# Two plain columns fewer and one Strassen step more in a two-layer diffusion backbone, with first columns in three passes and the softmax scale in the queries

## The chip, the cores and the metric

The kernel runs on one core of a Trainium2 chip. The metric is the device time of one execution in microseconds (us). Its engines work in parallel and each executes its own instruction stream: TensorE (PE) multiplies, VectorE (DVE) and ScalarE (ACT) work elementwise, GpSimd (POOL) issues some of the DMA transfers here, SyncE (SP) issues most. Semaphores order the engines among each other.

## The reference

Two layers. Each is a half-step gated FFN, a token mixing (a bidirectional mLSTM beside a multi-head latent attention), and a second half-step FFN; 256 context tokens and 256 latent tokens go through the same weights, D = 1024, hidden width 2816.

```python
def _swiglu(h, w_up, w_dn):
    a, b = jnp.split(h @ w_up, 2, axis=-1)
    return (jax.nn.silu(a) * b) @ w_dn
...
    def one(qi):
        s = jnp.einsum('bqhd,bkhd->bhqk', qi, k).astype(jnp.float32) * scale
        pr = jax.nn.softmax(s, axis=-1).astype(v.dtype)
        return jnp.einsum('bhqk,bkhd->bqhd', pr, v)
...
        mx = [m[:, None, :] for m in jnp.split(jax.nn.silu(c) @ w_ada[l] + b_ada[l], N_MOD, axis=-1)]
...
        x = x + 0.5 * mx[2] * _swiglu(_modulate(_rmsnorm(x, g_n1[l]), mx[0], mx[1]), w_ff1_up[l], w_ff1_dn[l])
```

## The kernel before

Everything is fp32. A product of two fp32 matrices is made of three matmuls on high and low parts: `hh`/`hl` are the parts of the normed activations, `wh`/`wl` those of a weight unit. ACT copies the unit `st` to `wh` (rounded), DVE subtracts to get `wl`. Four buffers exist for `wh` and `wl` each (`WB`), six for `st` (`STB`). A 256-wide matmul serves one of the two streams (CTX, LAT), a 512-wide one both.

The up projection of an FFN has 22 columns of 128 for each of the two halves a and b. In two of the four FFNs (`SEVEN`: layer 0's second, layer 1's first; function `ff7`) most columns are done two at a time as one *step*: a block product of a 2 x 2 matrix of weights (a11, a12, a21, a22) with the two streams' activations, by seven products instead of eight (class `Step`). Product r multiplies a combination of weights by a combination of activations. The combinations of activations (`d7`, their parts `dh` and `dl`) are made once per FFN by `differences`, on DVE (subtractions and low parts) and ACT (high parts). The combinations of weights are made per step: products 5, 6 and 7 add a further block onto the tile that is there by an accumulating DMA from POOL (`more`), and product 3 adds two tiles on DVE (`st_b += st_c`, where `st_c` is a21+a22+a11, product 6's tile). The products of one step are interleaved with two of the next, and the first step begins with (0,5), (0,1), (0,2), then (0,6), (1,5), (0,7), (0,3), where (t, r) is product r of step t. Their matmuls go into PSUM tiles `rA`, `rB`, `rC`, 24 of 256 each.

The first columns of an FFN come as plain ones. `up_early` does two of them stream by stream, as soon as the norm of a stream is there (LAT, then CTX); between them PE sums squares for the norm of the second stream (`nps`). Then `up` does the remaining plain columns (512 wide), and the steps follow. Finished columns go in chunks (`CHUNKS`: plain columns, steps) to the down projection (`dn`).

A queue of *ada* pieces (the modulation of later sub-layers: a weighted sum per row on DVE) is spread over the FFN by `drip`. A helper `high_priority(offset)` lets a scheduler put instructions earlier in their engines' streams; the streams themselves are then fixed, and each engine waits at an instruction until its semaphores are there.

Attention scores come as PSUM tiles `sc`; DVE takes the maximum of a row (L1470), scales it (L1471), ACT takes exp with the scale as its factor (L1475), DVE the reciprocal, ACT the division, and PE transposes the probabilities (`pT`).

Of the kernel before, what the change touches and what calls it, by code (L numbers as in the profile page):

```python
# [16 lines left out]
P = 128  # L17
D = 1024
KB = D // P
T = 512  # L20
# [24 lines left out]
FIRST = 4  # L45
STEPS = (FB - FIRST) // 2
CHUNKS = ((4, 1), (0, 4), (0, 4))
# [98 lines left out]
def body(ctx, tc, A):  # L146
# [178 lines left out]
    def silu2(out, src):  # L325

        tanh_half(out, src)
        V.scalar_tensor_tensor(out, out, 1.0, src, ALU.add, ALU.mult)

# [7 lines left out]
    def silu_rows(streams):  # L337

        res = {}
        for s in streams:  # L340
            for q in range(2):
# [3 lines left out]
                silu2(res[s, q], v)  # L345
# [243 lines left out]
    def up_early(part, jobs):  # L589
# [3 lines left out]
        banks = [(psum("pa"), psum("pb")) for _ in jobs]  # L593
        for b in (0, 1):
            for (lhs, _), pair_ in zip(jobs, banks):
                for i, ps in enumerate(pair_):
                    sl = slice(i * P, (i + 1) * P)
                    for k in range(KB):
                        for a in (0, 1) if b == 0 else (0,):
                            TE.matmul(  # L600
                                ps[:, :w], lhs[k][a][:, sl], hp[k][b],
                                start=b + k + a == 0, stop=b == 1 and k == KB - 1, skip_group_check=True,
                            )
                    flush()
        for (_, dst), (pa, pb) in zip(jobs, banks):
            gated(pa, pb, w, dst)
# [220 lines left out]
    def ff7(l, f, queue, after):  # L827
# [10 lines left out]
        for c, (first, n) in enumerate(CHUNKS):  # L838
# [20 lines left out]
            for st in mine:  # L859
# [23 lines left out]
    def mix(l, after):  # L883
# [530 lines left out]

        def mla_proj(p):
# [4 lines left out]
            run(split_gen([(a, b[:, :T], c[:, :T]) for a, b, c in zip(ps, his, los)]))  # L1420
# [4 lines left out]
            S.activation(z[:, :qn], ps[:, :qn], AF.Copy)  # L1425
# [26 lines left out]
        scale = (NOPE + ROPE) ** -0.5  # L1452

        def mla():
            def scores(p, hd, s):
# [322 lines left out]
```

## Time and profile before

| | |
|---|---|
| three runs | 2347.57, 2348.99, 2350.08 us; median 2348.99 |
| the profiled execution | 2347.62 us, span 2345.8 us, mean granted clock 0.993 |
| matmuls | 15414, PE busy 98% of the span |
| the two FFNs with steps | from 1021.8 to about 1375 and from 1375.7 to about 1734 |
| mixing of layer 0, of layer 1 | about 415 to 1000, 1734.6 to about 2141 |

A busy share is that of the whole span; a wait of PE is read from the list of waits and from the timeline around it. The lines L... are those of the kernel before.

### The profile page before, as it was taken

The numbers are of one execution on the slowest core, as the hardware profiler recorded it, in microseconds if no ns is written. First come the engines' busy times: TensorE is split into PE (matmuls) and PEld (weight loads), VectorE is DVE, ScalarE is ACT, GpSimd is POOL, SyncE is SP. The second block draws the span as 40 slices with busy tenths as digits, with TensorE's granted clock in tenths as the row PEclk, the third lists the DMA queues.
The fourth block names the chain that finished last, engine by engine and source line by source line (L and its number), as shares of the span: only waits on it lengthen the run. The fifth ranks groups of instructions, "written<-read, shape, count | busy, mean of one in ns | idle before, by whom it ended". The sixth has DMA issues, their size and how long they took to land.

```text
span 2345.8 us, 39386 instructions
## 1 busy us (share of the span) xinstructions
PE 2291.2 (98%) x15414; PEld 2083.6 (89%) x15414; DVE 1695.6 (72%) x3463; ACT 1089.9 (46%) x1776; POOL 144.1 (6%) x298
## 2 busy tenths in 40 slices
PE   8999999999999999999999999999999899999998
PEld 4888888888888888889999999999998798999998
DVE  6777777797477745468795868986878776776755
ACT  6322223567545433254443554443546564555443
POOL 1112110000010000000101000100000000000000
PEclk9999999999999999999999999999999999999999
DMA  9547444312122223436776637786732233365763
GB/s 337 200 155 239 153 150 151 102 57 73 55 81 73 73 77 94 128 105 185 203 218 166 193 89 212 213 253 183 239 94 83 91 100 99 99 183 161 245 206 105
DMA packets 116825, 347.15 MB, mean 148 GB/s; under 512 B 13854, under 2 KB 16158, under 8 KB 116638
## 3 DMA queue, kind: packets, MB, share of 16 engines
q1 hardware_dynamic: 99902, 286.94, 38.1%
q0 software_dynamic: 16736, 57.68, 10.9%
q8 instruction: 121, 1.98, 0.3%
q14 instruction: 66, 0.54, 0.1%
HBM read 341.42 MB, written 3.15 MB: 147 GB/s over the span
## 4 chain that ended last, share of the span: by engine, by line
PE 92%; DVE 4%; ACT 1%; DMA 1%; issue 1%; SPq 0%; DVEq 0%; ACTq 0%
PE dn L268 12%; PE dn L518 9%; PE rA L775 8%; PE p L292 4%; PE p L293 4%; PE p L294 4%; PE rB L775 4%; PE pa L294 3%; PE pa L292 3%; PE pa L293 3%; PE pb L292 3%; PE pb L294 3%; PE pb L293 3%; PE pv L268 2%; PE rC L775 2%; PE pb L600 2%
## 5 line engine op out<-in xcount | busy, mean ns | idle before, releaser
L246 ACT ACTIVATE wh<-st 128x1024 fp32r<-128x1024 f32 (+3 forms) x396 | 391.6, 993 | 641.3 <-PE pb L293 120.3
L248 DVE TENSOR_TENSOR wl<-st,wh 128x1024 fp32r<-128x1024 f32 (+3 forms) x396 | 449.6, 1139 | 201.3 <-ACT wh L246 198.0
L759 ACT ACTIVATE wh<-st 128x1024 fp32r<-128x1024 f32 x126 | 133.0, 1058 | 126.0 <-PE dn L518 54.2
L404 DVE SCALAR_TENSOR_TENSOR ada<-ada,cs 128x512 f32<-128x512 f32 x256 | 168.4, 686 | 18.7 <-DMA ada<-ada 18.7
L293 PE MATMUL p<-hl,wh 128*128 128x256 f32 (+1 forms) x536 | 179.4, 335 | 0.0
L292 PE MATMUL p<-hh,wh 128*128 128x512 f32 (+1 forms) x512 | 173.5, 339 | 0.0
L294 PE MATMUL p<-hh,wl 128*128 128x512 f32 (+1 forms) x512 | 172.5, 337 | 0.0
L760 DVE TENSOR_TENSOR wl<-st,wh 128x1024 fp32r<-128x1024 f32 x126 | 153.8, 1222 | 22.0 <-ACT wh L759 21.8
L512 DVE SCALAR_TENSOR_TENSOR x<-dn,mod,x 128x256 f32<-128x256 f32 x168 | 75.5, 479 | 96.8 <-PE dn L268 48.9
L404 DVE SCALAR_TENSOR_TENSOR junk<-ada,cs 128x512 f32<-128x512 f32 x192 | 124.2, 686 | 1.9 <-DMA ada<-ada 1.9
L294 PE MATMUL pb<-hh,wl 128*128 128x512 f32 (+1 forms) x352 | 120.6, 343 | 0.0
L294 PE MATMUL pa<-hh,wl 128*128 128x512 f32 (+1 forms) x352 | 120.6, 343 | 0.0
L292 PE MATMUL pa<-hh,wh 128*128 128x512 f32 (+1 forms) x352 | 120.6, 343 | 0.0
L292 PE MATMUL pb<-hh,wh 128*128 128x512 f32 (+1 forms) x352 | 120.6, 343 | 0.0
L293 PE MATMUL pa<-hl,wh 128*128 128x512 f32 (+1 forms) x352 | 120.4, 342 | 0.0
L293 PE MATMUL pb<-hl,wh 128*128 128x512 f32 (+1 forms) x352 | 120.4, 342 | 0.0
L293 PEld LDWEIGHTS p<-hl,wh 128*128 128x128 f32 x536 | 100.7, 188 | 10.8
L294 PEld LDWEIGHTS p<-hh,wl 128*128 128x128 f32 x512 | 96.1, 188 | 11.3
L292 PEld LDWEIGHTS p<-hh,wh 128*128 128x128 f32 x512 | 96.1, 188 | 10.9
L268 PE MATMUL dn<-hi,wh 128*128 128x512 f32 (+1 forms) x286 | 102.5, 360 | 0.0
L268 PE MATMUL dn<-hi,wl 128*128 128x512 f32 (+1 forms) x286 | 102.3, 358 | 0.0
L268 PE MATMUL dn<-lo,wh 128*128 128x512 f32 (+1 forms) x286 | 102.1, 358 | 0.0
(436 smaller groups left out, 7067.8 us busy)
## 6 DMA issues: line engine op xcount, KB each, us to landing
st<-wall SPq DMA_DIRECT2D x372, 512.0 KB, 3.7
ada<-ada SPq DMA_DIRECT2D x176, 256.0 KB, 5.9
ada<-ada POOLq DMA_DIRECT2D x112, 256.0 KB, 3.5
st<-wall POOLq DMA_DIRECT2D x54, 512.0 KB, 5.8
st<-wall SPq DMA_DIRECT2D x56, 384.0 KB, 3.4
st<-wall SPq DMA_DIRECT2D x32, 320.0 KB, 3.0
cb<-cc SPq DMA_DIRECT2D x14, 256.0 KB, 6.2
x<-xT SPq DMA_DIRECT2D x8, 256.0 KB, 5.6
```

What stands on the lines that cost most here:

```text
L246: S.activation(hi[:, :n], st[:, :n], AF.Copy)
L248: V.tensor_tensor(lo[:, :n], st[:, :n], hi[:, :n].bitcast(F32), ALU.subtract)
L268: TE.matmul(ps, lhs[k][a][:, lsl], rhs[k][b][:, rsl], start=i == 0, stop=i == 3 * n - 1)
L292: TE.matmul(ps, a, b, start=first, stop=False)
L293: TE.matmul(ps, a, bl, start=False, stop=False)
L294: TE.matmul(ps, al, b, start=False, stop=final_)
L404: V.scalar_tensor_tensor(o, st, 0.5, cb[s, q], ALU.mult, ALU.mult, accum_out=dst)
L512: V.scalar_tensor_tensor(xs[nb][:, cols], ps[:, pcols], mod(l, s, g, nb), xs[nb][:, cols], ALU.mult, ALU.add)
L518: TE.matmul(ps[:, s * HALF : (s + 1) * HALF], lhs[k][a], rhs[k][s][b], start=start and i == 0, stop=stop and i + 1 == len(todo), skip_grou ...
L759: S.activation(hi, st, AF.Copy)
L760: V.tensor_tensor(lo, st, hi.bitcast(F32), ALU.subtract)
L775: mm = TE.matmul(ps[:, p * HALF : (p + 1) * HALF], w[x][:, p, k], hx["op", r][k][y], start=new and i == 0, stop=i + 1 == len(todo), skip_g ...
```

## The change

Five edits. In the two FFNs with steps, two plain columns (`FIRST`) are left instead of four, all of them done by `up_early`, and ten steps instead of nine do the rest. `up_early` goes over its two columns in three passes (`hh` with `wh`, `hh` with `wl`, `hl` with `wh`) and keeps a and b of a column in one PSUM tile `pab`; the start of the mixing gets the same order. The weights by which `drip` spreads the ada pieces are changed. The softmax scale moves into the copies that make the query parts, so the scaling of the maximum (48 instructions) goes away, and reductions, exps and divisions get a raised priority. Silu of the conditioning goes through ACT's Silu table instead of tanh and a DVE operation.

```diff
-FIRST = 4
+FIRST = 2
 STEPS = (FB - FIRST) // 2
-CHUNKS = ((4, 1), (0, 4), (0, 4))
+CHUNKS = ((2, 2), (0, 4), (0, 4))
...
-                silu2(res[s, q], v)
+                silu(res[s, q], v)
...
-                V.scalar_tensor_tensor(o, st, 0.5, cb[s, q], ALU.mult, ALU.mult, accum_out=dst)
+                V.scalar_tensor_tensor(o, st, 1.0, cb[s, q], ALU.mult, ALU.mult, accum_out=dst)
...
-        banks = [(psum("pa"), psum("pb")) for _ in jobs]
-        for b in (0, 1):
-            for (lhs, _), pair_ in zip(jobs, banks):
-                for i, ps in enumerate(pair_):
-                    sl = slice(i * P, (i + 1) * P)
-                    for k in range(KB):
-                        for a in (0, 1) if b == 0 else (0,):
...
+        banks = [psum("pab") for _ in jobs]
+        order = [(a, b, n, i, k) for a, b in ((0, 0), (1, 0), (0, 1)) for n in range(len(jobs)) for i in (0, 1) for k in range(KB)]
+        for a, b, n, i, k in order:
+            TE.matmul(
+                banks[n][:, i * w : (i + 1) * w], jobs[n][0][k][a][:, i * P : (i + 1) * P], hp[k][b],
+                start=a + b + i + k == 0, stop=b + i == 2 and k == KB - 1, skip_group_check=True,
+            )
...
-                queue.run(min(1.0, done[0] / (STEPS + len(CHUNKS) * KB * 2 / 7 - 0.6)))
+                queue.run(min(1.0, done[0] / (STEPS * 0.6 + len(CHUNKS) * KB * 0.5 - 0.6)))
...
-                    drip(1 / 7)
+                    drip(0.6 / 7)
...
-                drip(2 / 7)
+                drip(0.5)
...
-            run(split_gen([(a, b[:, :T], c[:, :T]) for a, b, c in zip(ps, his, los)]))
+            run(split_gen([(a, b[:, :T], c[:, :T]) for a, b, c in zip(ps, his, los)], scale))
...
-                    mx.append(sp.tile([P, 3], F32, tag="mx", name="mx", bufs=8))
-                    V.reduce_max(mx[qb][:, 0:1], ps[qb], AX.X, negate=True)
-                    V.tensor_scalar(mx[qb][:, 0:1], mx[qb][:, 0:1], scale, None, ALU.mult)
-                    pump()
+                    with tc.high_priority(offset=SOON):
+                        mx.append(sp.tile([P, 3], F32, tag="mx", name="mx", bufs=8))
+                        V.reduce_max(mx[qb][:, 0:1], ps[qb], AX.X, negate=True)
+                        pr.append(act(F32, "pr")[:, :nk])
+                        S.activation(pr[qb], ps[qb], AF.Exp, bias=mx[qb][:, 0:1], accum_out=mx[qb][:, 1:2])
+                    pump(2)
```

In the changed kernel L600 is L591, L577/L580 (gating) are L572/L575, L695 to L697 (differences) L687 to L690, L682 (low part) L674, L752 (`st_b += st_c`) L744, L760 (`wl` of a product) L752, L775 (products) L767, L464 (`nps`) L459.

**The start of layer 0's second FFN on PE.** Of before, from the last pairs on the first early column to the first product; `pa` and `pb` are the two halves of a column, `hh`/`hl` and `wh`/`wl` the parts of activations and weights:

```order
L600 MATMUL pa<-hh,wh 128x256
L600 MATMUL pa<-hh,wl 128x256
L600 MATMUL pa<-hl,wh 128x256 x6
L464 MATMUL nps<-sq,ones 128x256 x2
L600 MATMUL pb<-hh,wh 128x256
...
L600 MATMUL pb<-hl,wh 128x256 x8
L292 MATMUL pa<-hh,wh 128x512
L293 MATMUL pa<-hl,wh 128x512
...
L294 MATMUL pb<-hh,wl 128x512
L775 MATMUL rC<-dh,wh 128x256
```

And of the change, from the end of the mixing to the first matmul of product (0,5):

```order
L268 MATMUL dn<-lo,wh 128x256
L591 MATMUL pab<-hh,wh 128x256 x16
L591 MATMUL pab<-hh,wl 128x256 x16
L591 MATMUL pab<-hl,wh 128x256 x6
L459 MATMUL nps<-sq,ones 128x256 x2
L591 MATMUL pab<-hh,wh 128x256 x16
L591 MATMUL pab<-hh,wl 128x256 x16
L591 MATMUL pab<-hl,wh 128x256 x26
L591 MATMUL pab<-hh,wh 128x256 x32
L591 MATMUL pab<-hh,wl 128x256 x32
L591 MATMUL pab<-hl,wh 128x256 x32
L767 MATMUL rC<-dh,wh 128x256
```

Ahead of `nps` stand 38 matmuls of the early columns (before: 16 in pairs and 6); behind `up_early` the 96 matmuls of 512 (L292 to L294) are gone, and product (0,5), which goes into `rC`, follows at once.

**The same place on DVE.** The numbers tell buffers apart. Of before, from the last gating of `up_early`: `st_10107`, `wl_10111` belong to product (0,5), `st_10147`, `wl_10150` to (0,1):

```order
L577 TENSOR_TENSOR sg_9920<-sg_9920,pb_9818 128x256
L695 TENSOR_TENSOR d7_9925<-h7_9514,h7_9667 128x512
L760 TENSOR_TENSOR wl_10111<-st_10107,wh_10110 128x1024
L580 TENSOR_TENSOR hl_9814<-sg_9920,hl_9814 128x256
L682 TENSOR_TENSOR dl_9928<-d7_9925,dh_9927 128x512
L695 TENSOR_TENSOR d7_9931<-h7_9521,h7_9674 128x512
L682 TENSOR_TENSOR dl_9934<-d7_9931,dh_9933 128x512
L696 SCALAR_TENSOR_TENSOR d7_9937<-d7_9925,h7_9681 128x512
L760 TENSOR_TENSOR wl_10150<-st_10147,wh_10149 128x1024
L682 TENSOR_TENSOR dl_9940<-d7_9937,dh_9939 128x512
L696 SCALAR_TENSOR_TENSOR d7_9943<-d7_9931,h7_9688 128x512
```

And of the change: `wl_9923` is product (0,5)'s, `wl_9962` is (0,1)'s, `wl_9995` is (0,2)'s and `wl_10027` is (0,6)'s; `st_9919` is `st_c` and `st_9992` is `st_b`:

```order
L752 TENSOR_TENSOR wl_9923<-st_9919,wh_9922 128x1024
L752 TENSOR_TENSOR wl_9962<-st_9959,wh_9961 128x1024
L752 TENSOR_TENSOR wl_9995<-st_9992,wh_9994 128x1024
L572 TENSOR_TENSOR sg_9865<-sg_9865,pab_9767 128x256
L575 TENSOR_TENSOR hl_9765<-sg_9865,hl_9765 128x256
L744 TENSOR_TENSOR st_9992<-st_9992,st_9919 128x1024
L572 TENSOR_TENSOR sg_9870<-sg_9870,pab_9768 128x256
L752 TENSOR_TENSOR wl_10027<-st_9919,wh_10026 128x1024
L687 TENSOR_TENSOR d7_9875<-h7_9472,h7_9615 128x512
L575 TENSOR_TENSOR hl_9766<-sg_9870,hl_9766 128x256
L674 TENSOR_TENSOR dl_9878<-d7_9875,dh_9877 128x512
L687 TENSOR_TENSOR d7_9881<-h7_9479,h7_9622 128x512
```

The three `wl` of the first products, the addition `st_b += st_c` of (0,3) (L744) and `wl` of (0,6) now stand ahead of the first difference (L687); before, the first difference stood ahead of the first `wl` of a step, and the same addition (L752) came 15 rows behind it. L744 waits for the landing of POOL's accumulating transfer for (0,6), and that transfer for `wl_9923`.

## Rows read from the trace of the kernel before

**Rows 1.** The page, parts 1 and 4: busy time, share and instructions; shares of the chain that ended last.

```profile
PE 2291.2 (98%) x15414; PEld 2083.6 (89%) x15414; DVE 1695.6 (72%) x3463; ACT 1089.9 (46%) x1776; POOL 144.1 (6%) x298
...
PE 92%; DVE 4%; ACT 1%; DMA 1%; issue 1%; SPq 0%; DVEq 0%; ACTq 0%
```

**Rows 2.** The list of PE's waits: who waited for whom, us in total, times, longest.

```profile
PE pT L1489 <- ACT pr L1475: 6.4, 1, 6.4
...
PE rB L775 <- DVE rB L812: 2.7, 2, 2.5
```

**Rows 3.** The chain that ended last, 1045 to 1160: start, us, what.

```profile
1048.63 0.93 PE pb L600 x8
...
1071.72 0.24 PE pb L294
1071.96 2.84 PE rC L775 x24
...
1083.23 2.84 PE rC L775 x24
...
1134.12 2.83 PE rA L775 x24
...
1153.85 2.83 PE rA L775 x24
```

**Rows 4.** Timeline of PE from 1014: start, us, instruction [idle before and its releaser].

```profile
1023.85 0.39 PE L600 MATMUL pa<-hh,wh 128*128 128x256 f32 x1 [0.84 <-ACT hh L672]
...
1027.86 0.78 PE L600 MATMUL pa<-hl,wh 128*128 128x256 f32 x2 [1.15 <-DVE hl L673]
1028.60 1.13 PE L464 MATMUL nps<-sq,ones 128*128 128x256 f32 x4
```

**Rows 5.** Windows: us, busy time of PE, PEld, DVE, ACT, POOL, granted clock, DMA, GB/s.

```profile
1383.00:1386.00 3.00, 3.00 (x15) 2.67 (x14) 0.64 (x2) 1.65 (x4) 0.00 (x0) 0.60 0.81 207
...
1820.00:1840.00 20.00, 13.55 (x84) 12.17 (x83) 19.56 (x42) 10.45 (x21) 1.52 (x3) 0.83 0.46 143
...
1836.00:1838.00 2.00, 2.00 (x8) 1.71 (x8) 1.97 (x8) 2.00 (x6) 0.00 (x0) 0.50 0.36 145
```

**Rows 6.** Timeline of ACT from 1044.

```profile
1047.26 2.01 ACT L246 ACTIVATE wh<-st 128x1024 fp32r<-128x1024 f32 x2 [3.33 <-PE pb L600]
...
1058.90 0.64 ACT L681 ACTIVATE dh<-d 128x512 fp32r<-128x512 f32 x1 [2.00 <-DVE d L695]
```

**Rows 7.** Timeline of DVE from 1044.

```profile
1057.24 0.42 DVE L580 TENSOR_TENSOR hl<-sg,hl 128x256 fp32r<-128x256 f32 x1
...
1058.18 0.69 DVE L695 TENSOR_TENSOR d<-h,h 128x512 f32<-128x512 f32 x1
1059.57 0.69 DVE L682 TENSOR_TENSOR dl<-d,dh 128x512 fp32r<-128x512 f32 x1 [0.70 <-ACT dh L681]
1060.18 0.69 DVE L696 SCALAR_TENSOR_TENSOR d<-d,h 128x512 f32<-128x512 f32 x1
1061.70 1.23 DVE L760 TENSOR_TENSOR wl<-st,wh 128x1024 fp32r<-128x1024 f32 x1 [0.84 <-ACT wh L759]
...
1069.65 1.22 DVE L752 TENSOR_TENSOR st<-st 128x1024 f32<-128x1024 f32 x1
```

**Rows 8.** Timeline of POOL from 1056.

```profile
1063.22 0.84 POOL L732 DMA_DIRECT2D st<-wall  x1 [4.50 <-DVE wl L760]
```

**Rows 9.** Line L732 alone (54 accumulating transfers): from issue to landing.

```profile
DMA to landing us min/median/max: 5.2/5.8/11.4
```

**Rows 10.** Timeline of DVE from 1826, layer 1's attention.

```profile
1830.83 0.69 DVE L1470 TENSOR_REDUCE mx<-sc 128x1 f32<-128x512 f32 x1
...
1831.94 0.69 DVE L1470 TENSOR_REDUCE mx<-sc 128x1 f32<-128x512 f32 x1
...
1834.76 0.21 DVE L1471 TENSOR_SCALAR mx<-mx 128x1 f32<-128x1 f32 x2
```

**Rows 11.** Timeline of ACT from 1828.

```profile
1834.94 0.69 ACT L1475 ACTIVATE pr<-sc,mx 128x512 f32<-128x512 f32 x1 [5.51 <-DVE mx L1471]
```

More of the change, by code (lines that the diff above doesn't have):

```diff
@@ L323, in silu @@
         S.activation(out, src, AF.Silu)
-    def silu2(out, src):
-        tanh_half(out, src)
-        V.scalar_tensor_tensor(out, out, 1.0, src, ALU.add, ALU.mult)
     mods = {}
@@ L592, in up_early @@
         w, hp = part.stop - part.start, hpairs(part)
-        banks = [(psum("pa"), psum("pb")) for _ in jobs]
-        for b in (0, 1):
-            for (lhs, _), pair_ in zip(jobs, banks):
-                for i, ps in enumerate(pair_):
-                    sl = slice(i * P, (i + 1) * P)
-                    for k in range(KB):
-                        for a in (0, 1) if b == 0 else (0,):
[L600 to L606, printed above, removed]
+        banks = [psum("pab") for _ in jobs]
[5 more added lines that the diff above has]
+            )
+            if k == KB - 1:
+                flush()
+        for (_, dst), ps in zip(jobs, banks):
+            gated(ps[:, :w], ps[:, w : 2 * w], w, dst)
     def ff(l, f, streams, queue, after):
@@ L1412, in mlstm @@
             heads[NH - 1].turn()
+        scale = (NOPE + ROPE) ** -0.5
         def mla_proj(p):
@@ L1424, in mla_proj @@
             z = act(F32, "qz")
-            S.activation(z[:, :qn], ps[:, :qn], AF.Copy)
+            S.activation(z[:, :qn], ps[:, :qn], AF.Copy, scale=scale)
             lhs = units([("ukv", l, p)], UW, 2)
@@ L1450, in mla_proj @@
             ready["mla", p] = pairs2(his, los), qr, [k[1:] for k in kn], [v[1:] for v in mv]
-        scale = (NOPE + ROPE) ** -0.5
         def mla():
@@ L1468, in scores @@
                 for qb in range(2):
[L1469 to L1479 removed]
+                    with tc.high_priority(offset=SOON):
[4 more added lines that the diff above has]
+                    pump(2)
+                for qb in range(2):
+                    with tc.high_priority(offset=SOON):
+                        V.reciprocal(mx[qb][:, 2:3], mx[qb][:, 1:2])
+                        S.activation(pr[qb], pr[qb], AF.Copy, scale=mx[qb][:, 2:3])
                     pump()
@@ L1534, in mix @@
             h_ = hpairs(cols)
+            outs = [(pk[:, cols], 1, two[1])]
             if cols == LAT or not last:
-                for b in range(3):
-                    mm3(pq[b][:, cols.start - q0 : cols.stop - q0], lhs[b // 2], h_, lsl=two[b % 2], late=True)
-                    if b == 1:
+                outs = [(pq[b][:, cols.start - q0 : cols.stop - q0], b // 2, two[b % 2]) for b in range(3)] + outs
+            for a, b in ((0, 0), (1, 0), (0, 1)):
+                for n, (o, u, sl) in enumerate(outs):
+                    for k in range(KB):
+                        TE.matmul(
+                            o, lhs[u][k][a][:, sl], h_[k][b],
+                            start=a + b + k == 0, stop=b == 1 and k == KB - 1, skip_group_check=True,
+                        )
+                    if n == 1:
                         flush()
-            mm3(pk[:, cols], lhs[1], h_, lsl=two[1], late=True)
         sq = lowrank_squares([t[:, :qn] for t in pq], qn)
@@ L1619, in body @@
     sc = cp.tile([P, 16], F32, name="sc")
-    silu2(sc, vecs[:, c0 : c0 + 16])
-    V.tensor_scalar(sc, sc, 0.5, None, ALU.mult)
+    silu(sc, vecs[:, c0 : c0 + 16])
     squares = [act(F32, "sq")[:, :T] for _ in range(KB)]
```

6 lines of the change are left out of this document (removed).

## Prediction

> **What bounds the kernel now.** I read the page first. TensorE (PE) is busy 98% of the span and carries 92% of the chain that ended last; VectorE (DVE) is busy 72% [rows 1]. So a term counts when it removes matmul time from PE, or when it opens or closes a wait of PE; work of the other engines counts only where PE ends up waiting for it. I then took the list of PE's waits. It is short: the largest single one is a transpose in layer 1's attention, 6.4 us, and the products of the FFNs wait for the rB addition 2.7 us in all [rows 2]. Almost nothing is idle, so the change can give little, and the question is which waits it creates. The chain and the timelines at the first of the two FFNs with seven products (it starts at 1021.8) give the rest.
>
> The profiled execution took 2347.62 us, 1.4 below the median of 2348.99. The sum is made against 2347.62 and the forecast is set against the median, so 1.4 is added at the end. About 0.2%, 4.7 us, is what a measurement of this kernel can tell from no change.
>
> **The change, part by part.**
>
> *A step for two plain columns.* The two plain columns run from the end of `up_early` (1048.63 + 0.93 = 1049.56) to the first product at 1071.96: 22.4 us for 96 matmuls of 512. One step is seven products, 1134.12 to 1153.85 = 19.73 us, 0.117 us a matmul (2.80 / 24) [rows 3]. Two FFNs: 2 x 2.67 = -5.3 us.
>
> *Three passes at the start of an FFN.* PE waits 0.84 us for hh, then 1.15 for hl, and reaches the norm's sums of the other stream (`nps`) at 1028.60 [rows 4]. When `nps` can start is set by its squares, not by PE. Before, 22 matmuls of the early columns stand ahead of `nps`; now 38 do (PE's order above), so 16 more, 16 x 0.117 = 1.9 us, are done while PE would wait. I take off 0.25 for the table load that now stands before the last hh on ScalarE (ACT): -1.65 each, -3.3 us for the two FFNs. Bounds: 0 if the wait only moves, -1.9 each if all is gained. In the second FFN the wait is followed by a spell at a mean granted clock of 0.60, part of it at the lower level of 1.2 GHz: 15 matmuls in 3 us instead of the 1.75 that they need [rows 5]. If PE stays busier it goes: -1.3, with 0 as the other bound.
>
> *The cover that the two plain columns gave.* This is the term that decides. Write E for the end of `up_early`. Before, DVE and ACT had the 22.4 us of the plain columns to build the differences (`d7`, `dh`, `dl`) and the step's weights (`wh`, `wl`). Now product (0,5) stands right behind `up_early`, and needs at E what was built over the next 22 us.
>
> Its weights can't be early. All four `wh` buffers hold the two early columns, and the row of before in which ACT converts the next ones waits 3.33 us for PE and starts at 1047.26, 2.3 before E [rows 6]. So wh of (0,5) is done about E-1.1, and its wl, 1.23 us on DVE, at E+0.2 [rows 7]. Then comes what the order shows: behind it stand wl of (0,1) and (0,2), two small gating operations, and at once the addition `st_b += st_c` of product (0,3) (L744), ahead of the differences. That addition waits for POOL's accumulating transfer of (0,6) into the same `st_c`, and this transfer may begin only when wl of (0,5) has read `st_c`. In the trace POOL issues 0.29 us after that wl ends (1061.70 + 1.23, then 1063.22) [rows 7, 8], and a transfer of this line lands 5.2 to 11.4 us after its issue, 5.8 in the median [rows 9]. I take the median: the lowest and the highest bound it. So: issue E+0.5, landing E+6.3, addition 1.22 to E+7.5, one gating operation 0.4 to E+7.9, wl of (0,6) 1.23 to E+9.1. Only then does d7 of (0,5) start: 0.6 for d7, 0.64 for dh on ACT, the rest of a gating operation and dl 0.69 to E+11.1, then the second half. From one d7 to the next takes 2.0 us when dl has to wait for dh (1058.18 to 1060.18) [rows 7]: second dl at E+13.0. Half of the 24 matmuls are still to come, 1.4: (0,5) ends at E+14.5 instead of E+2.8.
>
> (0,1), (0,2), (0,6) follow at 2.8 each, to E+22.9, no longer waiting. (1,5) waits again: its wl stands behind four more pairs of d7 and dl (4 x 2.0, to E+21.0), two d7 of product 4 (1.2), one low part (0.7), the addition into a7 (0.7) and takes 1.23, to E+24.9. (1,5) ends at E+27.7. In the trace of before it ends 14.1 after the first product begins (1083.23 + 2.84 - 1071.96) [rows 3]. Delay 13.6, which PE never regains, since it is the bound. What is behind the waiting addition on DVE is thus everything that PE needs next; POOL and SP have nothing late. The second FFN has the same order of rows. 2 x 13.6 = +27.2. Bounds: landing at 5.2 makes each 0.6 less, at 11.4 5.6 more; a DVE that is not held by the addition is a rival below.
>
> *ada pieces.* The queue of modulation pieces is spread by weights; products had 9 of 15.3 and have 6 of 17.4 now, so less of it falls where DVE also makes the weights. The 2.7 us for rB should go [rows 2]: -2.7, 0 at the other end (the stretches of the down projection get more of it, and there PSUM banks lie between DVE and PE).
>
> *Softmax.* The 6.4 us are one transpose that needs a PSUM bank that exp frees. The exp waits 5.51 us for the scaling of the maximum: both maxima are there at 1832.63, the two scalings run at 1834.76, behind other work of a DVE that is busy 19.56 of 20 us [rows 5, 10, 11]. Now no scaling stands between, and the first exp could begin at the end of its own reduction, 1830.83 + 0.69 = 1831.52 instead of 1834.94: -3.4. The bounds are 0 (another operation stands there) and -8 (the wait and the spell at 0.50, 1.2 GHz, behind it, 8 matmuls in 2.0 us [rows 5]). Layer 0's attention has only small waits: -1, between -4 and +2, since raised priority of reductions and exps also pushes something else back.
>
> *Mix start, silu, scale.* In layer 0, 7 matmuls fewer stand ahead of `nps`: 7 x 0.117 = +0.8; 0 in layer 1. Silu by table instead of tanh, and the scale in a copy that runs anyway, sit on ACT and DVE away from PE's waits: 0, within 0.5 either way.
>
> Sum: -5.3 - 3.3 - 1.3 + 27.2 - 2.7 - 3.4 - 1.0 + 0.8 = +11.0. 2347.62 + 11.0 + 1.4 = 2360.0.
>
> By the Trainium skill (DMA: Bandwidth & Descriptors, the section Anatomy of one DMA) a transfer from GpSimd takes about 2.0 us and its bytes at 436 GB/s, an estimated 3.2 us for these 512 KB. The stall would be 2.6 shorter in each FFN and the time about 2355; no transfer of this line landed under 5.2 in the trace, and the page's fit is of plain copies, so the trace's median stays in the sum.
>
> **The rivals.**
>
> *A. DVE is not held by the waiting addition.* If it went on to d7 behind it, d7 would start at about E+3.6 (two more wl and two gating operations after E+0.2), the second dl would be at E+7.6, and (1,5) would end near E+22.2: a delay of 8 each, 16 in all, against -16.2 of the other terms: 2349, no change. Against it: the dl at 1059.57 waits 0.70 us for ACT while the next d7 at 1060.18, whose inputs were complete, stands behind it [rows 7]. The Trainium skill (Perfetto Trace Analysis, Tensor Engine Instruction) calls ACT, DVE and GPSIMD "strict FIFO"; by that rule, with which the row agrees, this rival is left only as a chance that the wait itself is shorter than I think.
>
> *B. The stall is hidden, and the kernel is faster.* Its place is the same: conversion and differences would have to be over before E. Without any stall the sum is -16.2, so 2332.8; it ends faster by over 0.2% if the stall is below 5.7 us in each FFN. That needs wh of (0,5) to start some 10 us sooner; the ACT row that waits for PE's last reading of a buffer speaks against it [rows 6].
>
> *C. The stall is worse.* Landing at 11.4 [rows 9], or the rB addition ahead of (0,3) late behind ada pieces, adds 5 to 6 us per FFN: above 2371.
>
> **How the numbers follow.** Forecast 0.68, A 0.12, B 0.12, C 0.08. The time is the forecast's, 2360. The range leaves out B and C: from 2345, which takes in A, to 2371. Faster: B and a quarter of A, 0.15. Within 0.2%: the rest of A and a little of the forecast's lower edge, 0.11. Slower: 0.74.
>
> **What would show it.** In the profile after: a wait of PE at the first L767 in both FFNs for dh or dl, 9 to 13 us in all, and one of 1 to 3 us at (1,5) for wl; a DVE idle of 2 to 4 us ahead of L744, put down to a DMA; no PE wait for rB; the transpose's 6.4 shortened. If PE passes from `up_early` to rC with under 3 us idle, the decisive term is wrong and B holds. The prediction also fails if the attention stretches move by more than 8 us either way.

## The result and the profile after

The changed kernel takes 2372.78 us (median of 2371.60, 2371.81, 2373.76 and 2375.98), against 2348.90 for the kernel before in the same series: ratio 1.0095, 95% interval [1.0083, 1.0107], which is 22.3 us (19.5 to 25.1); the medians are 23.9 apart. The sign was forecast, the size was not: +11.0 in the sum, and 2371 as the upper end of the range.

The profiled execution took 2373.76 us (span 2372.1, mean granted clock 0.985, was 0.993). The page, parts 1 and 4, as in [rows 1]:

```profile
PE 2301.6 (97%) x15558; PEld 2099.4 (89%) x15558; DVE 1696.2 (72%) x3413; ACT 1099.7 (46%) x1788; POOL 149.1 (6%) x304
...
PE 88%; DVE 4%; issue 3%; DMA 2%; ACT 2%; POOL 0%; DVEq 0%; SPq 0%; POOLq 0%; ACTq 0%
```

PE has 10.4 us more of busy time, and its share of the chain falls from 92 to 88%. The busy time can't come from the work: it has two plain columns fewer and one step more in each of two FFNs, which is less matmul time. The same work was done at a lower clock in more places. The list of PE's waits, against [rows 2], has the idle part:

```profile
PE rC L767 <- ACT dh L673: 19.5, 2, 9.9
...
PE pT L1480 <- ACT pr L1465: 3.0, 1, 3.0
PE rA L767 <- ACT sa L795: 2.8, 2, 1.6
...
PE rB L767 <- DVE rB L804: 0.4, 1, 0.4
```

Two new waits of nearly 10 us stand at the first product of the two FFNs with steps; the transpose's wait halved, and the one for rB (2.7) is down to 0.4. Cut at the starts of the same stages on PE (first matmul of a kind in the trace), the two spans differ so:

| stretch on PE | before | after | difference |
|---|---|---|---|
| span's start to first early column, layer 0's first FFN | 42.9 | 44.2 | +1.3 |
| its early columns | 24.2 | 26.2 | +2.0 |
| rest of that FFN | 348.0 | 348.0 | 0.0 |
| mixing of layer 0 | 606.7 | 607.5 | +0.8 |
| layer 0's second FFN (steps) | 353.9 | 366.5 | +12.6 |
| layer 1's first FFN (steps) | 358.9 | 366.4 | +7.5 |
| mixing of layer 1 | 412.1 | 413.9 | +1.8 |

Where the stall stands, PE has only two waits between the early columns and the end of (1,5). Timeline of PE, from 1052:

```profile
1063.41 0.58 PE L767 MATMUL rC<-dh,wh 128*128 128x256 f32 x1 [9.87 <-ACT dh L673]
...
1075.85 0.39 PE L767 MATMUL rA<-dh,wh 128*128 128x256 f32 x1 [1.60 <-ACT sa L795]
```

`up_early` ends at 1063.41 - 9.87 = 1053.54; this is E. The timeline of POOL, the one of DVE and the one of ACT behind it:

```profile
1053.87 0.85 POOL L724 DMA_DIRECT2D st<-wall  x1 [25.49 <-DVE wl L752]
```

```profile
1056.80 0.43 DVE L575 TENSOR_TENSOR hl<-sg,hl 128x256 fp32r<-128x256 f32 x1 [0.48 <-ACT hl L574]
1059.40 1.23 DVE L744 TENSOR_TENSOR st<-st 128x1024 f32<-128x1024 f32 x1 [2.17 <-DMA st<-wall]
...
1060.88 1.22 DVE L752 TENSOR_TENSOR wl<-st,wh 128x1024 fp32r<-128x1024 f32 x1
1062.01 0.69 DVE L687 TENSOR_TENSOR d<-h,h 128x512 f32<-128x512 f32 x1
```

```profile
1059.40 1.06 ACT L751 ACTIVATE wh<-st 128x1024 fp32r<-128x1024 f32 x1 [2.36 <-DMA st<-wall]
...
1062.73 0.63 ACT L673 ACTIVATE dh<-d 128x512 fp32r<-128x512 f32 x1 [1.32 <-DVE d L687]
```

The reader sees the chain of the forecast link by link. The transfer is issued at E+0.3 and both engines go on at 1059.40, E+5.9, with DVE idle for 2.17 us at an addition whose result PE needs six products later. d7, whose inputs are complete, starts behind it at E+8.5. In layer 1 the same row of PE stands at 1428.12 with 9.67 us.

The stall costs more than its two waits. PE comes out of the first one at half clock, and the 24 matmuls of (0,5) take 5.1 us where they took 2.84 before:

```profile
1064.00:1067.00 3.00, 2.86 (x13) 2.86 (x14) 1.98 (x4) 0.92 (x2) 0.00 (x0) 0.50 0.89 310
```

The rest of the 26 us between the two spans is in no list of waits. Windows, columns as in [rows 5]; the first piece is the kernel before (early columns of layer 0's first FFN, start of its mixing), the second the changed kernel in the same stages (they stand 1.3 and 3.4 us later there) and at the start of layer 0's second FFN:

```profile
45.00:48.00 3.00, 3.00 (x18) 3.00 (x18) 3.00 (x9) 3.00 (x6) 0.00 (x0) 0.61 1.02 393
48.00:51.00 3.00, 3.00 (x28) 3.00 (x27) 3.00 (x9) 2.37 (x6) 1.51 (x3) 1.00 0.81 284
...
423.00:426.00 3.00, 3.00 (x28) 3.00 (x28) 2.90 (x9) 0.78 (x2) 0.00 (x0) 1.00 0.00 0
```

```profile
45.00:48.00 3.00, 3.00 (x10) 2.37 (x10) 3.00 (x9) 3.00 (x8) 0.00 (x0) 0.50 1.03 397
48.00:51.00 3.00, 3.00 (x18) 3.00 (x17) 3.00 (x9) 3.00 (x7) 0.69 (x2) 0.60 0.85 321
...
423.00:426.00 3.00, 3.00 (x16) 3.00 (x16) 3.00 (x7) 0.00 (x0) 0.00 (x0) 0.52 0.48 150
...
1030.00:1034.00 4.00, 4.00 (x24) 4.00 (x23) 3.56 (x8) 2.83 (x8) 0.00 (x0) 0.57 0.99 267
```

PE counts as busy for the whole length of each of them, but at a granted clock of 0.50 to 0.60, in whole or in large part at the lower of its two levels (1.2 GHz), 3 us hold 10 to 18 matmuls where they hold 28 at 1.00. A busy share doesn't show this; the count and the clock beside it do. The clock isn't the only cause: the 10 in the changed kernel's first window are matmuls that wait for one hh each, and these come 0.4 us apart.

One trace doesn't price an order of matmuls, because these spells at half clock also come and go between executions and between the two FFNs of one execution. The early columns of the FFNs with steps, with PE's order there alike within a row of the table, took over all the profiled runs of this case (from the first matmul to the end of the last, us):

| order of the early columns | clock at 1.00 behind the norm's wait | with a spell at half clock |
|---|---|---|
| of the kernel before | 27.75 (2 times) | 29.0 to 29.4 (5 times), 30.4 (once, a longer spell) |
| three passes | 25.9 to 26.0 (13 times) | 27.4 to 27.7 (7 times) |

The kernel before had such a spell in layer 1 and none in layer 0, the changed kernel the other way round. A spell costs about 1.5 us in either order. That accounts for most of the difference between +12.6 and +7.5 in the table of stretches.

### The profile page after: what moved, and what is told of

Read it like the earlier page. It is cut to its first block, busy times and chain, and to the rows that moved or that the text cites. A ratio compares the mean times of both kernels' runs of the same rounds, so it can differ in the third digit from the quotient of the medians.

```text
span 2372.1 us, 39653 instructions
## 1 busy us (share of the span) xinstructions
PE 2301.6 (97%) x15558; PEld 2099.4 (89%) x15558; DVE 1696.2 (72%) x3413; ACT 1099.7 (46%) x1788; POOL 149.1 (6%) x304
## 4 chain that ended last, share of the span: by engine, by line
PE 88%; DVE 4%; issue 3%; DMA 2%; ACT 2%; POOL 0%; DVEq 0%; SPq 0%; POOLq 0%; ACTq 0%
PE dn L268 11%; PE dn L513 9%; PE rA L767 8%; PE rB L767 4%; PE p L292 4%; PE p L293 4%; PE p L294 4%; PE pa L293 2%; PE pb L293 2%; PE pa L292 2%; PE pb L292 2%; PE pa L294 2%; PE pb L294 2%; PE pv L268 2%; PE rC L767 2%
## 5 line engine op out<-in xcount | busy, mean ns | idle before, releaser
L751 ACT ACTIVATE wh<-st 128x1024 fp32r<-128x1024 f32 x140 | 146.7, 1056 | 142.9 <-PE dn L513 48.7
L752 DVE TENSOR_TENSOR wl<-st,wh 128x1024 fp32r<-128x1024 f32 x140 | 170.5, 1222 | 35.0 <-ACT wh L751 34.5
L399 DVE SCALAR_TENSOR_TENSOR ada<-ada,cs 128x512 f32<-128x512 f32 x256 | 168.6, 688 | 26.1 <-DMA ada<-ada 25.8
L292 PE MATMUL p<-hh,wh 128*128 128x512 f32 (+1 forms) x512 | 173.4, 339 | 0.0
L294 PE MATMUL p<-hh,wl 128*128 128x512 f32 (+1 forms) x512 | 172.5, 337 | 0.0
L293 PEld LDWEIGHTS p<-hl,wh 128*128 128x128 f32 x536 | 100.7, 188 | 10.9
L513 PE MATMUL dn<-gh,wh 128*128 128x256 f32 x544 | 108.7, 281 | 0.0
L513 PE MATMUL dn<-gh,wl 128*128 128x256 f32 x544 | 108.5, 281 | 0.0
L513 PE MATMUL dn<-gl,wh 128*128 128x256 f32 x544 | 108.4, 280 | 0.0
L293 PE MATMUL pa<-hl,wh 128*128 128x512 f32 (+1 forms) x320 | 108.0, 337 | 0.0
L294 PE MATMUL pa<-hh,wl 128*128 128x512 f32 (+1 forms) x320 | 107.9, 337 | 0.0
L294 PE MATMUL pb<-hh,wl 128*128 128x512 f32 (+1 forms) x320 | 107.9, 337 | 0.0
L292 PE MATMUL pa<-hh,wh 128*128 128x512 f32 (+1 forms) x320 | 107.8, 337 | 0.0
L292 PE MATMUL pb<-hh,wh 128*128 128x512 f32 (+1 forms) x320 | 107.8, 337 | 0.0
L294 PEld LDWEIGHTS p<-hh,wl 128*128 128x128 f32 x512 | 96.1, 188 | 11.3
L292 PEld LDWEIGHTS p<-hh,wh 128*128 128x128 f32 x512 | 96.1, 188 | 11.0
```

Source lines behind the costliest of these rows:

```text
L292: TE.matmul(ps, a, b, start=first, stop=False)
L293: TE.matmul(ps, a, bl, start=False, stop=False)
L294: TE.matmul(ps, al, b, start=False, stop=final_)
L399: V.scalar_tensor_tensor(o, st, 1.0, cb[s, q], ALU.mult, ALU.mult, accum_out=dst)
L513: TE.matmul(ps[:, s * HALF : (s + 1) * HALF], lhs[k][a], rhs[k][s][b], start=start and i == 0, stop=stop and i + 1 == len(todo), skip_grou ...
L751: S.activation(hi, st, AF.Copy)
```

## The experiments

All times are compared with runs of the kernel before on the same chip (medians 2350.45 to 2351.0 us; three chips). A ratio of 0.001 is 2.35 us. "Cover" below means that work of DVE and ACT is done while PE has other matmuls.

**The two edits with a size, undone and alone.** First the changed kernel with the old columns, all other edits kept:

```diff
-FIRST = 2
+FIRST = 4
-CHUNKS = ((2, 2), (0, 4), (0, 4))
+CHUNKS = ((4, 1), (0, 4), (0, 4))
```

> The changed kernel with four plain columns and nine steps again; passes, drip, softmax and silu stay as changed. Cover theory (PE waits because the first step's weights and the differences are made after the early columns, with nothing to cover them): the wait ahead of the first product goes in both FFNs, 2 x 14.1 of delay comes back and 2 x 2.7 of step saving is lost, so 2372.8 - 28.2 + 5.3 = 2350, between 2346 and 2354. Rival (most of the 24 us lies in the other edits, through the clock of TensorE): no more than half comes back, 2360 or above.

Measured: 2346.64, ratio 0.9982 [0.9973, 0.9991]. The loss is gone, so the columns cause it. The four other edits give -4.2 us (-6.3 to -2.1) together; the forecast had -10.9 for them (-3.3 - 1.3 - 2.7 - 3.4 - 1.0 + 0.8).

Then the columns alone, on the kernel before (the same two lines the other way round):

> The kernel before with one part of the change alone: two plain columns and ten steps instead of four and nine, with the drip's old weights. Theory of the cover: +27.2 for the two stalls and -5.3 for the step, +22, 2371, range 2367 to 2376, with waits of TensorE at the first product of both FFNs of 8 to 13 us. Rival (the stall needs the other edits too, the table load of silu or the three passes, to be this long): under 2362.

Measured: 2375.60, ratio 1.0098 [1.0084, 1.0113], +23.0 us (19.7 to 26.6), against -5.3 + 27.2 = +21.9 in the forecast. Its waits at the first products (the profiled execution was the fastest of the four, 2369.69):

```profile
PE rC L775 <- ACT dh L681: 16.7, 2, 8.4
...
PE rC L775 <- DVE dl L682: 1.7, 2, 0.8
```

Neither the three passes nor Silu's table nor the drip is needed for the stall. The first line is 2.8 below the changed kernel's 19.5, but here each wait for dh is followed by one for dl. From the end of the early columns to the end of (1,5) it is 27.4 and 27.8 us, against 28.1 and 28.0 in the changed kernel: the passes lengthen the stall by 0.8 us in both FFNs together.

**The shared tile alone.** In the first step product (0,6) gets weights of its own (three transfers into a new tile), so that its last transfer doesn't have to wait for (0,5)'s `wl`:

```diff
+                elif r == 6 and self.t == 0:
+                    self.fresh("e", "a21")
+                    self.more("e", "a22")
+                    st = self.more("e", "a11")
...
-                    V.tensor_tensor(st, st, self.st["c"], ALU.add)
+                    V.tensor_tensor(st, st, self.st["c" if self.t else "e"], ALU.add)
```

> The changed kernel, but the weights of product (0,6) are summed in a tile of their own by three transfers that need not wait for the low parts of (0,5); two more transfers per FFN, order of the differences unchanged. If the landing of POOL's transfer is what holds the start (the landing theory), its 5.9 us vanish and the differences begin some 6 us sooner: 2372.8 - 2 x 6 = 2361 or less. If the differences are late mainly because they stand behind four low parts, an addition and two gatings on VectorE (the order theory), they begin at E+6.5 instead of E+8.5: 2372.8 - 2 x 2 = 2369.

Measured: 2365.00, ratio 1.0062 [1.0047, 1.0077], between the two expectations. The waits at the first products:

```profile
PE rC L771 <- ACT dh L673: 15.2, 2, 7.6
```

d7 starts at E+6.2 instead of E+8.5, nearly as expected (6.5), and still far too late: without the transfer, the addition and the weights of the next products are still ahead of it on DVE. By the waits (19.5 to 15.2) the landing is about a quarter of the stall, the order of DVE the rest.

**The order of DVE, first try.** Differences 5 to 7 are written ahead of the second stream's early columns, 4 behind product (0,2):

```diff
                     up_early(part, [(lhs, gs[i][s]) for i, lhs in early])
+                    if s:
+                        rest = differences()
+                        next(rest)
                     if s and queue:
                         queue.begin()
-                rest = differences()
-                next(rest)
...
                     mark = steps[u].product(r, mark)
+                    if (u, r) == (0, 2):
+                        next(rest, None)
```

> The changed kernel with the differences of products 5, 6 and 7 written ahead of the context stream's early columns, and those of product 4 behind product (0,2); the landing of the transfer for (0,6) is still waited for. Cover theory: (0,5) can start at E+0.2 when its weights are there, and the next thing late is the copy sa on ScalarE behind the high part of (0,6), at about E+15, so (1,5) ends near E+21 instead of E+28: 2372.8 - 2 x 7 = 2359, between 2354 and 2364. Rival (only the weights matter, not the differences): 2370 or more.

And the same with the own tile for (0,6):

> Both together: differences early and a tile of its own for product (0,6). Cover theory: no engine waits for the landing, (0,6) starts near E+10 and (1,5) ends near E+16, against E+14.1 with no wait at all: 2372.8 - 2 x 12.5 = 2348, between 2344 and 2354. If something else at the start holds PE (the weight buffers, the clock after idle), no better than e3.

Measured: 2370.31, 1.0081 [1.0066, 1.0096], and 2368.61, 1.0074 [1.0057, 1.0091]: two misses. In both, (0,5) starts right behind the early columns, as meant, and the stall moves: the lists of PE's waits, first run and second run, each with one line,

```profile
PE rA L767 <- ACT sa L795: 23.9, 2, 12.1
```

```profile
PE rA L771 <- ACT sa L799: 21.8, 2, 11.3
```

put it at (0,6), which needs a PSUM bank that ACT copies out (`sa`). ACT's timeline in the second run has the reason:

```profile
1065.69 0.63 ACT L323 ACTIVATE cs<-cb 128x512 f32<-128x512 f32 x1 [3.99 <-DMA cb<-cc]
...
1071.24 0.58 ACT L799 ACTIVATE sa<-rA 128x512 f32<-128x512 f32 x1
```

A Silu of the conditioning, needed much later, stands ahead of `sa` on ACT and waits for its row (3.76 us in the first run). My reordering had moved the load of that row on SP's queue from 1032 to 1060, behind a weight load that waits for a buffer. The trap was of the same kind as the change's: one late transfer, and an engine that takes its work in order.

**The order mended.** Differences 5 and 6 ahead of the second stream's early columns, 7 behind (0,2), 4 behind (1,5), the conditioning's Silu in place (one buffer less, loads as early as in the changed kernel), and the own tile:

```diff
-                res[s, q] = act(F32, "cs")[:, :512]
-                silu(res[s, q], v)
+                res[s, q] = v
+                silu(v, v)
...
-            if r == 4:
+            if r in (7, 4):
...
+                    if s:
+                        rest = differences()
+                        next(rest)
...
+                    if (u, r) in ((0, 2), (1, 5)):
+                        next(rest, None)
```

> The changed kernel with the order of the work around the early columns mended: differences 5 and 6 of the first step are written ahead of the CTX early columns, 7 behind product (0,2), 4 behind (1,5); the condition's silu is written in place so that no ScalarE work waits for a second buffer; (0,6) of the first step has a weight tile of its own. Theory of the cover (the stall is order on VectorE and ScalarE, not a lack of engine time): the first product starts right behind the early columns and no wait of TensorE over 2 us is left before (1,5); the changed kernel's 2372.8 less two delays of 13.6 is about 2346, range 2342 to 2352. Rival (the work itself doesn't fit under the early columns, so that the stall moves to the next product again, as in the two runs before): 2365 to 2372, with a wait of 8 us or more at rA or rB.

Measured: 2344.08, ratio 0.9970 [0.9958, 0.9982], 28.7 us under the changed kernel by the medians (which are of different chips; 29 by the ratios) and faster than the kernel before. The list of waits has no line for rC and dh any more; the largest lines of the products that are left are

```profile
PE rA L771 <- ACT sb L799: 3.7, 4, 1.1
...
PE rA L771 <- DVE wl L756: 1.3, 1, 1.3
...
PE rA L771 <- ACT sa L799: 0.8, 2, 0.4
```

From the first early column to the end of (1,5) it is 42.3 and 42.2 us, about 2 more than the early columns and five products take without any wait (26.0 + 14.1); the changed kernel took 55.6 and 54.0. So nearly all the work of DVE and ACT fits under the early columns and the first products. What stalled PE was the order, not a lack of engine time.

The same without the own tile:

> The mended order with three passes, without the own tile: (0,6) takes its weights from the shared tile st_c again, so that the addition of (0,3) waits for the transfer of (0,6) on VectorE as in the changed kernel. Theory that the order of the differences alone is the cover: the waiting addition now has products (0,5) and (0,1), (0,2) ahead of it on TensorE, the delay is about 2 us in each FFN, +4 against the mended kernel, about 2350. Theory that the shared tile and the waiting addition are the cause: the stall comes back with over 7 us in each FFN, +14 or more.

Measured: 2349.61, ratio 0.9992 [0.9983, 1.0001], +5.2 us against the mended order (by the ratios; the two ran on different chips). The addition still waits 2.53 us on DVE for the transfer (at 1055.69), but three products now stand before the next wait of PE:

```profile
1061.21 0.39 PE L767 MATMUL rA<-dh,wh 128*128 128x256 f32 x1 [3.01 <-ACT sa L795]
```

The shared tile is worth about 2.6 us in each FFN (from the first early column to the end of (1,5): 44.9 and 44.5 instead of 42.3 and 42.2); the order of the differences, with the Silu in place that it needs, is worth the rest.

**The other edits, one at a time on the kernel before.** Three passes in the early columns and at the mixing's start:

> The kernel before with one part of the change alone: three passes, highs first, in the early columns and at the mix's start. The forecast's theory (matmuls moved ahead of a wait are gained): -3.3 for the two FFNs, -1.3 for the half-clock spell, +0.8 at the mix: -3.8, about 2345. Theory of the clock (what stays ahead is done one hh at a time, TensorE falls to the lower clock or stays there longer): +2.0 in the first FFN, +2.7 at the mix of layer 0, -0.2 and -3.1 in the FFNs of the changed order, as in the trace of the changed kernel: +1.4, about 2350.

Measured: 2350.09, ratio 0.9997 [0.9988, 1.0006], -0.7 us (-2.8 to +1.4): nothing that can be told from no change, and not the forecast's -3.8, which lies outside the interval. In its trace the first FFN's early columns are again +2.3. The early columns of the two FFNs with steps are 26.0 and, with a spell at half clock, 27.7.

The scale in the queries and the raised priorities:

> The kernel before with one part of the change alone: the scale in the copies of the queries, the maxima unscaled, and the raised priority of reductions, exps and normalisations. The forecast's theory: the transpose's wait of 6.4 us falls by 3.4, and 1 more in layer 0: -4.4, about 2344.6. Theory of the clock: the wait of the transpose falls by 3.4, but TensorE leaves the wait at half clock and stays there, and small waits take the place: 0 to +0.5, about 2349.

Measured: 2348.64, ratio 0.9993 [0.9984, 1.0002], -1.6 us (-3.8 to +0.5), between the theories. Layer 0's mixing is 1.5 shorter and layer 1's 0.3. PE's rows at the transpose of the changed kernel show what takes the place of the wait:

```profile
1856.92 1.12 PE L1480 MATMUL pT<-consts,pr 128*128 128x128 f32 x4 [3.02 <-ACT pr L1465]
...
1861.91 0.80 PE L268 MATMUL kn<-hi,wh 128*128 128x512 f32 x1 [0.87 <-DVE vl L976]
```

and the windows there:

```profile
1856.00:1858.00 2.00, 1.08 (x4) 0.72 (x4) 1.91 (x4) 1.91 (x6) 0.00 (x0) 0.51 0.30 123
...
1862.00:1864.00 2.00, 2.00 (x5) 1.61 (x6) 2.00 (x4) 0.60 (x1) 0.00 (x0) 0.50 0.00 0
1864.00:1866.00 2.00, 2.00 (x6) 1.52 (x6) 1.33 (x3) 0.00 (x0) 0.00 (x0) 0.50 0.00 0
```

PE comes back 3.4 us sooner, at half clock, catches up with DVE, waits for `vl`, and is at half clock for about 10 us; before, it waited longer and then had its clock back after about 4. PE's next long wait, at `s` (a product of the mLSTM, L268), stands 243.1 us behind the start of the mixing in the kernel before and 243.4 in the changed one: nothing of the 3.4 is left. In the run of these edits alone, PE has the same wait at the transpose (2.96) and two behind it (0.53 and 0.87), but its clock back some 5 us sooner, and the wait at `s` stands at 241.2: 1.9 are left. There its clock falls once more, 0.50 for a spell that costs 1.5 us; 10 of the 11 profiled runs with these edits have one there, and none of the 3 without. Why the edits bring it isn't shown.

**Which place pays for three passes.** The mended order without them, and then with them only in the two FFNs with steps (the other FFNs and the mixing as in the kernel before):

```diff
                 for part in (LAT, CTX) if len(streams) == 2 else (LAT,):
-                    up_early(part, [(lhs, at(gs[i], part)) for i, lhs in early])
+                    up_plain(part, [(lhs, at(gs[i], part)) for i, lhs in early])
```

> The mended order (differences 5 and 6 ahead of the CTX early columns, silu in place, own tile for (0,6)), but without the three passes: early columns and the mix's start in the order of the kernel before. The forecast's theory (three passes are worth 3.8 in all): 3.8 slower than the mended kernel with passes. Theory of the clock, stage by stage: -2.4 in the first FFN and -1 to -3 at the two mixes, +2 and +1.5 to 3 in the two FFNs with seven products, where the passes do what was forecast: within 2 us of the mended kernel with passes.

> The mended order, with three passes only in the early columns of the two FFNs with seven products; the other FFNs and the mix's start in the order of the kernel before. Theory of the clock: the passes gain 2 and 1.5 to 3 us where the norm's wait follows the early columns, and lose 2.4 in the first FFN and 1 to 3 at the mixes, so this is the fastest: 3 to 5 us under the mended kernel with passes everywhere, about 2340. The forecast's theory (gain in both kinds of place but the mix): within 1 us of it.

Measured: 2346.16, ratio 0.9976 [0.9965, 0.9987] without them, which can't be told from having them everywhere; and 2342.03, ratio 0.9956 [0.9943, 0.9968] with them in the two places only. The traces agree in sign with what was expected by stage: without passes the first FFN's early columns take 24.1 instead of 26.6 us and the two mixings 2.6 less in all, while the early columns of the two FFNs with steps take 29.2 and 28.9 (to the first product) instead of 25.8 each. About 1.5 of each of the last two differences is a spell at half clock, which this run has in both FFNs and the mended kernel in neither; the mixed kernel has it in one (27.5 and 25.8). The mixed kernel has the lowest time of all that ran, 10.3 us (7.5 to 13.4) under the kernel before; that it beats the mended order with passes everywhere (7.1, 4.2 to 9.9) is not shown, since the intervals overlap. Its page and its first mixing, where 28 matmuls in 3 us are back:

```profile
PE 2288.2 (98%) x15558; PEld 2089.1 (89%) x15558; DVE 1695.9 (73%) x3413; ACT 1098.9 (47%) x1788; POOL 150.8 (6%) x306
```

```profile
424.00:427.00 3.00, 3.00 (x28) 3.00 (x28) 2.93 (x8) 1.61 (x4) 0.00 (x0) 1.00 0.00 0
```

It does the same 15558 matmuls as the changed kernel in 13.4 us less of busy time.

**Filler matmuls, to test the clock by itself.** In the first FFN's first group of the mended order, between one hh and the next:

```diff
+            if fill and a + b + n + i == 0:
+                for _ in range(fill if k else 0):
+                    w0 = jobs[0][0][0][0]
+                    TE.matmul(banks[1][:, :w], w0[:, :P], hp[k - 1][0], start=True, stop=True, skip_group_check=True)
```

> The mended order with three passes, and in the first FFN two filler matmuls of 256 columns between one hh and the next in the first group (14 in all), written to a bank that the next group overwrites. TensorE has 1.6 us more work at full clock and nothing less. Theory of the clock (three passes cost time there because single matmuls, one to an hh, leave TensorE at the lower clock until dense work has gone on for a while): the clock is back at about 47.5 to 48.5 us instead of 51, the early columns take about 24.5 instead of 26.6 us, -2 us in all. Rival (the time goes to waiting for hh, and the clock doesn't matter): 0 to +1.6 in this stage.

Measured: 2345.61, ratio 0.9972 [0.9961, 0.9984], the same as without. The windows of the mended kernel, and then of the one with fillers:

```profile
45.00:48.00 3.00, 3.00 (x11) 2.46 (x11) 3.00 (x9) 3.00 (x7) 0.65 (x2) 0.50 1.01 391
48.00:51.00 3.00, 3.00 (x16) 3.00 (x16) 3.00 (x9) 3.00 (x8) 1.49 (x3) 0.50 1.03 391
```

```profile
45.00:48.00 3.00, 3.00 (x16) 3.00 (x16) 3.00 (x9) 3.00 (x6) 1.08 (x2) 0.51 1.02 395
48.00:51.00 3.00, 3.00 (x27) 3.00 (x27) 3.00 (x9) 3.00 (x8) 1.07 (x2) 1.00 1.04 392
```

The clock rises 3 us sooner, near 48 as expected. That the fillers did it is not shown: the second run of the first try at DVE's order has the same matmuls here without fillers, its spell is no longer (it starts later), and its stage takes the same 25.8. Its window:

```profile
48.00:51.00 3.00, 3.00 (x21) 3.00 (x21) 3.00 (x9) 3.00 (x7) 0.87 (x2) 0.73 0.84 314
```

In the other direction, two runs with the order of the kernel before had a longer spell here and took 25.1 instead of 24.1 to 24.2. So over all runs a longer or shorter spell makes up to 1.0 us of this stage. The larger part is the order itself. With fillers the clock is back as early as in the kernel before, and the stage still takes 25.8 against 24.2. By the time of the eighth hh, 2.9 us after the first matmul, the kernel before has begun 17 of the stage's matmuls, four for each hh, the kernels with passes 8 (fillers not counted); nine matmuls at 0.117 us are 1.05. The expected gain was 2 us and 0.8 came; the fillers run at the lower clock themselves, 0.21 us apart, and hold up the matmuls behind them. The time of the whole can't tell 0.8.

## Why the prediction was right in sign and wrong in size

**What bounds the kernel: right.** Terms counted when they opened or closed a wait of PE, and the decisive one did. But "when it removes matmul time from PE, or when it opens or closes a wait of PE" left out a third thing: the clock at which PE does the same matmuls. The forecast priced it behind two waits only.

**Step and cover, -5.3 + 27.2: right, the exact size in part by luck.** 21.9 forecast, +23.0 (19.7 to 26.6) in the run of the columns alone. The links for the first of the two FFNs: landing 5.5 us after the issue at 1053.87 (forecast 5.8; 5.3 in the second FFN), d7 at E+8.5 (9.1), end of (1,5) at E+28.25 (27.7), a delay of 14.1 (13.6). By the Trainium skill (DMA: Bandwidth & Descriptors, Anatomy of one DMA) the estimate had been 3.2; here the two transfers took 5.5 and 5.3, so the trace's median was the better choice; the section says nothing of transfers that accumulate. Three details were off. The chain had PE wait for the second dl and then do half of the 24 matmuls at full clock; in the trace PE hardly waits there (0.14), because it does most of the 24 at half clock; (0,5) ends at E+15.0 instead of E+14.5 although d7 came 0.6 sooner. The second wait is not at (1,5) for wl but at (0,6) for `sa`, 1.6 us, which is queued on ACT behind other work; the wl of (1,5) is there in time. And the text said 9 to 13 us of waiting "in all" at the two first products, where its own chain gives about 10 in each; 9.9 and 9.7 came.

**Three passes, -3.3 - 1.3, and mix start +0.8: the first step that failed.** Together -3.8 was forecast; alone on the kernel before, the passes measured -0.7 (-2.8 to +1.4). The step was to count the matmuls that move ahead of a wait in two FFNs and to put the first FFN, which has the same `up_early`, at nothing. There the order that helps elsewhere hurts: hh's come 0.4 us apart, and the passes have one matmul for each where the order before had four. The stage takes 25.8 to 26.8 in all runs with passes against 24.1 to 25.1 without, +2.0 in the changed kernel.

At the mixing's start of layer 0 the +0.8 was too small. From its first matmul to the first of `ckv`, 24.6 to 24.7 us became 25.8 with the clock at 1.00 throughout, +1.2, and 26.8 to 27.3 in the three of nine runs with a spell at half clock. The changed kernel's profile is one of these, +2.7, which the faster softmax of layer 0 hides in the stage's +0.8.

In the two FFNs with steps the gain of -1.65 each came, spell compared with spell and without with without: 27.75 to 26.0, and 29.0 to 29.4 to 27.4 to 27.7. No row shows the 0.25 that was taken off for a table load; with Silu's table and without it the stage takes the same 25.96 and 25.97. The -1.3 for the spell in the second FFN was a reading of one execution: it went there in the changed kernel's profile and came in the first FFN with steps. Whether passes make spells rarer (7 of 20, against 6 of 8) isn't shown.

**Softmax, -3.4 - 1.0: its mechanism right, its size wrong, the second step that failed.** The first exp no longer waits for the scaling and the transpose's wait fell by 3.4, as worked out. The step that failed is that a shorter wait is a gain of the same length: waits of 0.9 to 1.4 us behind the transpose, one for `vl` among them, and half clock there or further on took its place. Alone it measured -1.6 (-3.8 to +0.5), against -4.4. Layer 0's -1 was about right, -1.5 in one trace.

**Ada pieces, -2.7:** PE's wait for rB went from 2.7 to 0.4, as forecast; with the old columns and the new weights of `drip` no line for rB is left, with the new columns and the old weights 1.0. The drip was not run by itself. What the four other edits give in all, -4.2 (-6.3 to -2.1), less passes and softmax, leaves -1.9 for drip and Silu, with an uncertainty of some 3.7, so no gain from them is shown.

**The sum with measured terms.** +23.0 - 4.2 = +18.8, against the +22.3 (19.5 to 25.1) of the ratio. The 3.5 between them lie within the intervals of the terms. Of the 11.3 us by which +22.3 exceeds the forecast's +11.0, the columns are 1.1 and the other edits 6.7 (-4.2 instead of -10.9), 3.1 of it the passes and 2.8 the softmax; the rest is not told apart from noise.

**The rivals.** A, a DVE that isn't held, falls: DVE is idle for 2.17 us at L744 while the next rows' inputs are complete. The Trainium skill (Perfetto Trace Analysis, Tensor Engine Instruction) calls the engine's queue strict FIFO, and this row agrees. B, a hidden stall, was wrong for this kernel, but the mended order shows that it can be had without what the text asked for, a wh some 10 us sooner: there wh of (0,5) starts at 1048.92, about 2 before E (1051.0), as in [rows 6], and its first products hardly wait, because the differences moved out of its way. Its time was put at 2332.8; the mended kernel took 2344.1, so the other terms failed there too. C had the time right, above 2371, and the reason wrong: the transfer landed early in its range, and what was missing were gains that did not come.

## What to carry to other kernels

Before removing work from the bounding engine, list what the other engines do behind it, and write that work where its inputs become ready rather than where it is used; one in-order engine with a waiting instruction at its head stops everything behind it, and mending one queue can move the late transfer to the next (SP's load, ACT's Silu). Price a moved matmul or a shortened wait only together with the clock that PE has there: read the number of matmuls in a window beside the granted clock, since busy time hides it, and read the stage in several executions, since a spell at half clock (1.5 us here) comes and goes. When an order moves to a new one, price it in every place that uses it: three passes gained about 1.6 to 1.8 us where a norm's wait followed and cost 1.2 to 2.4 where single matmuls met single inputs.

## What the runs showed of the hardware

I had not expected that PE's granted clock would differ so much between executions of the same matmuls. In the first FFN all profiled runs come out of a wait of 1.74 us and are at 0.50 behind it, most of them from about 1 us later. The kernel before (18 matmuls in 45 to 48) is back at 1.00 for all of 48 to 51; the mended kernel (11, then 16) is at 0.50 until 51; with fillers it is back at 1.00 from 48. But a run without fillers was back sooner as well, and two runs with the order of the kernel before stayed longer at 0.50. At the transpose the kernel before waited 6.4 us and was at 0.50 for about 7, partly while it still waited; the changed kernel waited 3.0 and then 0.87 and was at 0.50 for about 10, and the run of the softmax edits alone, with the same waits, for about 3. What decides how long a spell lasts is not shown here; what one costs is, 1.5 us in the early columns.
